# Projecting the first two token blocks of a hybrid attention layer one block at a time

## The chip, the cores and the metric

The kernel runs on one NeuronCore of a Trainium2 chip. The metric is the device time of one execution in microseconds (us). The program is one long, straight list of instructions for each engine: TensorE (PE; its weight loads are listed as PEld), VectorE (DVE), ScalarE (ACT), GpSimd (POOL) and the queue of SyncE (SP), which issues every transfer between memory and the chip.

## The reference

One layer of an encoder is applied to 2048 prompt tokens and 32 sample tokens. Its first half is what matters here:

```python
z = rmsnorm(x, g_attn) @ w_in            # 1024 -> 3072 columns
qa, ka, va, qb, kb, vb = split(z)        # group A: 512 columns each; group B: 512 columns each
oa = diff_attn(qa, ka, va, t5_bias, lam) # 4 heads, two maps of 64, values of 128, causal by chunks of 64
ob = band_attn(qb, kb, vb, clip_bias)    # 8 heads of 64, the own chunk of 64 and the 8 before it
h = x + concat(rms(oa), rms(ob)) @ w_out
```

After it come a squared-ReLU MLP, a gated per-layer embedding and a last norm. The sample tokens attend to 128 cached keys and to themselves. The new keys and values are outputs too.

## The kernel before

**Blocks.** The tokens lie in four blocks: blocks 0, 2 and 3 of 512 tokens, and block 1 of 512 prompt tokens and the 32 sample tokens. `HALVES` is [(0, 1), (2, 3)]. Every product is formed from values split in a high and a low part, as three matmuls (`mm3`, L211 to L213: high by high, high by low, low by high), accumulated over eight slices of 128 rows.

**`prep`** (L342) loads 128 tokens, squares and sums them, transposes them through PE (tiles `rp` and `xp`), scales them, stores `xT`, and writes the high and low halves `aH` and `aL` of the block, which stay on the chip until both groups have been projected.

**`wunit`** (L197) fetches one slice of weights of 512 KB (tile `wr`, two buffers) and splits it: ACT copies the high part `wh` (L189) and POOL subtracts the low part `wl` in four pieces of 256 columns (L184). `wh` and `wl` have three buffers each.

**`proj(half, grp, ...)`** (L381) projects the blocks in `half` for one group. It first takes two column slices of values, each of two weight units (PSUM tile `vps`; result through `vraw` and `vhl` to `vS`), and then for each of four `g` one slice of queries and one of keys (PSUM tile `qps`; results `qh`, `ql` to the scratch tensors `qS` and `kS` in memory). Its loops are ordered so:

```python
for c in vs:
    u = [self.wunit(wv[:, 4 * i : 4 * i + 4], [4, 256]) for i in range(2)]
    for b in half:
...
for g in gs:
    for kind in range(2):
        wh, wl = self.wunit(W[:, col : col + P].rearrange("(k p) c -> p k c", p=P), [8, P])
        for b in half:
```

So a slice is fetched and split once for each call, and serves all blocks of `half`. Keys are also transposed back for the output (`knat`, tile `ktp`, L471 and L480), in PSUM tiles that the argument `tp` gives: the call for group A passes the ring `ps_t`, the other calls pass the pool `mm`, which has two tiles and holds `vps` and `qps` too.

**`lam` and `biases`** (L254, L270) make lambda and the bias tables: two products on PE (tiles `pa`, `pb`), then rows written to memory and spread there to 128 rows for each head (`dba`, `dbb`).

**`attn_a(js, ...)`** (L534) is the attention of group A for the pairs of 128-query tiles in `js`; pair `j` covers tokens 256j to 256j + 255, and 8 stands for the sample tokens. For each head it loads the bias, the keys `ka` and the queries `q` from the scratch tensors, forms scores (`s`, L594), the softmax on DVE and ACT, transposes the weights through PE (`tpp`, L666) and multiplies by the values (`o`, L680 to L682). `JA0` is [(0, 1), (2, 3, 8)]: pairs 0 and 1 lie in block 0; pairs 2 and 3 and the samples lie in block 1 and see the keys of both blocks. `caches` (L491) brings the cached keys and values into the scratch tensors (tiles `ckn`, `ckh`, `ckl`) and must be done before the sample tokens.

**The order.** `run` (L1403) is traced in the order of its lines. A planner then puts the instructions of each engine in a fixed order: it runs a model of the engines in time, and whenever an engine is free it gives it the earliest instruction in the program whose inputs are ready by the model. So later work fills gaps of earlier work as far as its buffers are free, but on the chip each engine, and the SP queue, goes through its list strictly in that order. The part in question, L1433 to L1450, is: `prep` of blocks 0 and 1; `proj` of group A for both blocks; `lam` and `biases`; then `attn_a` for (0, 1), `caches`, `attn_a` for (2, 3, 8); then `proj` of group B for block 0, and after it for block 1, woven with `prep` of block 2. `prep` of block 2 is lifted to the rank that the program has at `mark` (L1443), but needs the buffers of block 0's activations.

Of the kernel before, what the change touches and what calls it, by code (L numbers as in the profile page):

```python
# [43 lines left out]
HALVES = [(0, 1), (2, 3)]  # L44
# [47 lines left out]
def drain(gen):  # L92
    for _ in gen:
        pass
# [57 lines left out]
class Kern:  # L152
# [1250 lines left out]
    def run(self):  # L1403
        tc, nc, a = self.tc, self.nc, self.a
        with ExitStack() as top:

            def opened(stack, name, bufs, space=None, side="left"):
                kw = {} if space is None else {"space": space}
                return stack.enter_context(
                    tc.tile_pool(name=name, bufs=bufs, side=side, reuse_waits="tile", **kw)  # L1410
                )
# [8 lines left out]
            mm = opened(psx, "mm", MM, PSUM)  # L1420
            tp = mm
            ps_s = opened(psx, "pss", 5 - MM, PSUM, "right")
            ps_t = opened(psx, "pst", 2, PSUM, "right")
# [4 lines left out]
            sg = opened(s12, "sg", 2)  # L1428
            self.consts(cp)
            with ExitStack() as x:  # L1430
                pp = opened(x, "pp0", 3, side="right")
                acts = {b: self.actpair() for b in HALVES[0]}
# [1 line left out]
                    drain(self.prep(b, acts, pp, ps_s, "s"))  # L1434
            ppx = ExitStack()
            pp = opened(ppx, "pp", 1)
            drain(self.proj(HALVES[0], 0, acts, sg, mm, Rings((ps_t, "tp"))))
            with ExitStack() as x:
                wk = opened(x, "setup", 1, side="right")
                self.lam(cp, wk)  # L1440
# [3 lines left out]
            with ExitStack() as x:  # L1444
                pool = opened(x, "a0", 1, side="right")
                for js in JA0:
                    if 8 in js:
                        self.caches(sg, tp)
                    self.attn_a(js, pool, ps_s, ps_t, ps_o)
            drain(self.proj((0,), 1, acts, sg, mm, tp))  # L1450
# [194 lines left out]
```

## Time and profile before

| quantity | value |
|---|---|
| median of 3 runs | 3224.73 us (3218.40 to 3230.53) |
| the profiled execution, its own time | 3224.94 us |
| span of the profile | 3223.1 us |
| granted TensorE clock, mean | 0.974 |
| busy: DVE, ACT, POOL | 1813.4, 1791.5, 1768.7 us |
| bytes moved | 579.89 MB, 180 GB/s over the span |

The profiled execution takes 1.84 us longer than its span, from the first to the last instruction. "Idle before" in a row of the profile is the time in which the engine waited ahead of that group of instructions, with the instruction or transfer whose end released it. In the rows by stretch, each engine has its busy microseconds and its count of instructions; PEclk is the granted clock of TensorE as a share of full speed; the DMA share is the mean busy share of the core's 16 DMA engines.

### The profile page before, as it was taken

Reading aid. Unit: us, or ns where it says so; the run is one execution under the profiler, and the core shown is the slowest. Engines: PE = TensorE matmul, PEld = TensorE weight load, DVE = VectorE, ACT = ScalarE, POOL = GpSimd, SP = SyncE. Lnnn points to the kernel's source line nnn. Section 1 sums busy time; section 2 is a strip of 40 time slices with the busy share of each in tenths; the row PEclk is TensorE's granted clock in tenths of the full one; section 3 lists DMA queues with packets and bytes.
Section 4 is the critical chain, followed back from the end, with each engine's and each line's share of the span. In section 5 each row is a group of like instructions: output and inputs, shape, how many; then the busy total and the mean of one; then the engine's idle time right before and its main releaser. Section 6 shows DMA issues by size and latency. Waiting matters only on the chain.

```text
span 3223.1 us, 51787 instructions
## 1 busy us (share of the span) xinstructions
PE 3019.3 (94%) x17497; PEld 2639.9 (82%) x17497; DVE 1813.4 (56%) x4270; ACT 1791.5 (56%) x3966; POOL 1768.7 (55%) x2451
## 2 busy tenths in 40 slices
PE   7989898999989999999999999998899999999997
PEld 6967788879878888788889999887788887888875
DVE  5126765444455454676675676235466665755845
ACT  4226665666566675676676776334354454444543
POOL 5427657443234544565564445657465567677751
PEclk9989899999999999999999999999999999999998
DMA  7578676987687854654564534456444468675611
GB/s 218 182 198 233 191 210 197 256 235 218 187 243 212 240 146 123 158 174 136 146 190 134 138 110 135 131 163 196 133 153 148 158 242 287 203 253 186 219 58 53
DMA packets 556257, 579.89 MB, mean 180 GB/s; under 512 B 41900, under 2 KB 412912, under 8 KB 555992
## 3 DMA queue, kind: packets, MB, share of 16 engines
q1 hardware_dynamic: 555992, 576.58, 59.7%
q8 instruction: 139, 2.28, 0.3%
q14 instruction: 126, 1.03, 0.1%
HBM read 438.37 MB, written 142.01 MB: 180 GB/s over the span
## 4 chain that ended last, share of the span: by engine, by line
PE 63%; DMA 11%; DVE 9%; ACT 4%; POOL 2%; issue 2%; SPq 1%; DVEq 0%; POOLq 0%; ACTq 0%
PE xps L211 3%; PE xps L212 3%; PE xps L213 3%; PE ups L211 3%; PE ups L212 3%; PE ups L213 3%; PE dps L211 3%; PE s L594 3%; PE dps L212 3%; PE dps L213 3%; PE dp L211 2%; PE dp L213 2%; PE dp L212 2%; PE ob L800 2%; PE gps L213 2%
## 5 line engine op out<-in xcount | busy, mean ns | idle before, releaser
L184 POOL TENSOR_TENSOR wl<-wr,wh 128x256 fp32r<-128x256 f32 x776 | 580.6, 780 | 463.3 <-ACT wh L189 405.4
L189 ACT ACTIVATE wh<-wr 128x1024 fp32r<-128x1024 f32 x258 | 272.6, 1057 | 259.4 <-PE dps L212 40.3
L211 PE MATMUL dps<-uh,wh 128*128 128x272 f32 (+1 forms) x768 | 265.4, 346 | 35.6 <-DVE h L982 27.7
L174 POOL TENSOR_TENSOR wl<-wr,wh 128x256 fp32r<-128x256 f32 x256 | 193.6, 787 | 170.5 <-ACT wh L189 170.3
L211 PE MATMUL ups<-cH,wh 128*128 128x272 f32 (+1 forms) x768 | 250.6, 327 | 2.7 <-ACT sqacc L913 1.5
L213 PE MATMUL dps<-uh,wl 128*128 128x272 f32 (+1 forms) x768 | 252.0, 328 | 0.0
L212 PE MATMUL dps<-ul,wh 128*128 128x272 f32 (+1 forms) x768 | 252.0, 328 | 0.0
L212 PE MATMUL ups<-cL,wh 128*128 128x272 f32 (+1 forms) x768 | 249.8, 325 | 1.2 <-POOL cL L174 1.2
L213 PE MATMUL ups<-cH,wl 128*128 128x272 f32 (+1 forms) x768 | 250.2, 326 | 0.0
L982 DVE TENSOR_TENSOR h<-h,dps 128x272 f32<-128x272 f32 (+1 forms) x384 | 195.9, 514 | 90.9 <-PE dps L213 88.7
L211 PE MATMUL qps<-aH,wh 128*128 128x512 f32 (+1 forms) x640 | 229.3, 358 | 8.8 <-DVE a L368 3.6
L213 PE MATMUL qps<-aH,wl 128*128 128x512 f32 (+1 forms) x640 | 229.0, 358 | 0.0
L212 PE MATMUL qps<-aL,wh 128*128 128x512 f32 (+1 forms) x640 | 228.5, 357 | 0.0
L594 PE MATMUL s<-ka,q 128*128 128x512 f32 (+3 forms) x768 | 188.9, 350 | 37.0 <-ACT e L608 19.3
L211 PEld LDWEIGHTS dps<-uh,wh 128*128 128x128 f32 x768 | 148.5, 193 | 60.6 <-DVE h L982 40.0
L608 ACT ACTIVATE e<-s,nm 128x384 f32<-128x384 f32 (+3 forms) x256 | 154.6, 609 | 64.5 <-DVE nm L600 42.6
L600 DVE TENSOR_REDUCE nm<-s 128x1 f32<-128x512 f32 (+3 forms) x256 | 147.4, 587 | 61.1 <-PE s L594 60.0
L212 PE MATMUL dp<-dx,dw 128*128 128x512 f32 x448 | 177.5, 396 | 0.7 <-DVE dx L195 0.7
L174 POOL TENSOR_TENSOR dw<-dv,dw 128x256 fp32r<-128x256 f32 x160 | 149.2, 961 | 49.1 <-ACT dw L189 39.8
L211 PE MATMUL dp<-dx,dw 128*128 128x512 f32 x448 | 174.7, 396 | 0.0
L594 PEld LDWEIGHTS s<-ka,q 128*128 128x128 f32 x768 | 128.3, 196 | 54.3 <-ACT e L608 24.3
L213 PE MATMUL dp<-dx,dw 128*128 128x512 f32 x448 | 171.5, 396 | 0.0
(273 smaller groups left out, 9593.9 us busy)
## 6 DMA issues: line engine op xcount, KB each, us to landing
wd<-w_down SPq DMA_DIRECT2D x96, 512.0 KB, 5.4
wr<-w_in SPq DMA_DIRECT2D x74, 512.0 KB, 5.5
q<-qS SPq DMA_DIRECT2D x256, 128.0 KB, 4.1
v<-vSa SPq DMA_DIRECT2D x64, 512.0 KB, 4.4
wr<-w_up SPq DMA_DIRECT2D x64, 512.0 KB, 4.3
wr<-w_down SPq DMA_DIRECT2D x64, 512.0 KB, 4.0
ut<-uS SPq DMA_DIRECT2D x56, 512.0 KB, 4.1
ka<-kS SPq DMA_DIRECT2D x32, 512.0 KB, 8.0
```

Of the source, the lines that this page charges most:

```text
L174: nc.gpsimd.tensor_tensor(out[:, sl], a[:, sl], b[:, sl], op=op)
L184: nc.gpsimd.tensor_tensor(out[:, sl], a[:, sl], b[:, sl], op=op)
L189: nc.scalar.activation(hi, raw, AF.Copy)
L211: nc.tensor.matmul(ps, lh, rh, start=start and i == 0, stop=False)
L212: nc.tensor.matmul(ps, lh, rl, start=False, stop=False)
L213: nc.tensor.matmul(ps, ll, rh, start=False, stop=stop and i == n - 1)
L594: nc.tensor.matmul(s, q[:, m, hl, P * qi : P * qi + nr], kt[:, m, k0 - kb : k0 - kb + n], start=hl == 0, stop=hl == 1)
L600: nc.vector.tensor_reduce(nmx, s, axis=AX.X, op=ALU.max, negate=True)
L608: nc.scalar.activation(dst, src, AF.Exp, bias=nmx, accum_out=z[:nr, m, bi : bi + 1])
L800: nc.tensor.matmul(o[:, qa:qb], vt, pt[:kn, i - kfirst, qa:qb], start=x == 0 and y == 0, stop=x == len(order) - 1 and y == 1,)
L982: nc.vector.tensor_tensor(hv, hv, ps, op=ALU.add)
```

## The change

The one call of `proj` for group A on both blocks becomes two calls of one block each. The call for block 0 stays where the old one was. The call for block 1 stands after the first attention, (0, 1), has been issued, ahead of `caches`, and passes `tp` (the pool `mm`) for the transposed keys. Every weight slice of group A is thus fetched and split once for block 0 and once more for block 1: 12 units (four of values, four of queries, four of keys) come in a second time.

```diff
             ppx = ExitStack()
             pp = opened(ppx, "pp", 1)
-            drain(self.proj(HALVES[0], 0, acts, sg, mm, Rings((ps_t, "tp"))))
+            drain(self.proj((0,), 0, acts, sg, mm, Rings((ps_t, "tp"))))
             with ExitStack() as x:
                 wk = opened(x, "setup", 1, side="right")
                 self.lam(cp, wk)
...
                 for js in JA0:
                     if 8 in js:
+                        drain(self.proj((1,), 0, acts, sg, mm, tp))
                         self.caches(sg, tp)
                     self.attn_a(js, pool, ps_s, ps_t, ps_o)
             drain(self.proj((0,), 1, acts, sg, mm, tp))
```

## What was predicted

> **What bounds the kernel now.** I read the page first, for the bound of the whole.
>
> ```profile
> span 3223.1 us, 51787 instructions
> PE 3019.3 (94%) x17497; PEld 2639.9 (82%) x17497; DVE 1813.4 (56%) x4270; ACT 1791.5 (56%) x3966; POOL 1768.7 (55%) x2451
> PE 63%; DMA 11%; DVE 9%; ACT 4%; POOL 2%; issue 2%; SPq 1%; DVEq 0%; POOLq 0%; ACTq 0%
> ```
>
> PE is busy for 94% of the span and no other engine for more than 56%. The edit changes no matmul: each weight slice meets the same columns of activations, only in two visits. So PE's work stays, and the time can change only by PE's idle time, by its clock, or by other engines that make it wait. I therefore asked for the stretches in which the moved work lies.
>
> ```profile
> core 0: us, PE busy (x) PEld busy (x) DVE busy (x) ACT busy (x) POOL busy (x), PEclk, DMA share, GB/s
> 0.00:20.00 20.00, 6.81 (x30) 5.94 (x30) 8.73 (x32) 12.18 (x31) 8.16 (x17) 1.00 0.79 234
> 20.00:40.00 20.00, 15.07 (x114) 14.19 (x112) 14.72 (x44) 11.62 (x33) 15.90 (x22) 1.00 0.93 295
> 40.00:60.00 20.00, 16.07 (x116) 15.16 (x117) 15.46 (x52) 8.73 (x25) 13.28 (x19) 0.90 0.59 183
> 60.00:180.00 120.00, 118.95 (x799) 109.72 (x799) 18.68 (x46) 28.37 (x53) 52.03 (x78) 0.99 0.53 172
> 180.00:200.00 20.00, 15.87 (x83) 10.38 (x81) 3.56 (x7) 3.68 (x7) 7.87 (x13) 0.91 0.60 190
> 200.00:220.00 20.00, 16.91 (x137) 16.27 (x138) 1.90 (x4) 4.74 (x8) 3.33 (x6) 1.00 0.99 260
> 220.00:240.00 20.00, 11.67 (x53) 9.78 (x51) 10.50 (x53) 9.81 (x37) 5.25 (x9) 0.59 0.79 193
> 240.00:320.00 80.00, 75.63 (x429) 64.96 (x429) 51.30 (x184) 51.71 (x156) 56.69 (x82) 0.98 0.84 234
> 320.00:400.00 80.00, 62.78 (x436) 58.39 (x436) 63.08 (x193) 55.90 (x170) 48.50 (x70) 0.87 0.68 191
> 400.00:540.00 140.00, 127.32 (x967) 120.81 (x966) 97.78 (x318) 96.64 (x289) 86.94 (x142) 0.99 0.70 201
> 540.00:560.00 20.00, 15.79 (x66) 12.39 (x65) 7.15 (x16) 6.21 (x12) 17.08 (x27) 0.91 0.68 206
> ```
>
> There are four stages. Until 60 us the two blocks are prepared, and PE idles 13.19 + 4.93 + 3.93 = 22.05 us. From 60 to 180 us PE runs projection alone and is full. From 180 to 240 us comes a passage to the attention, with 4.13 + 3.09 + 8.33 = 15.55 us idle. From 240 to 540 us attention and group B's projection mix, with 4.37 + 17.22 + 12.68 = 34.27 us idle.
>
> That decides how the edit must be judged. It moves block 1's projection out of the full stage and uses it to fill the attention. But the attention is filled already, by group B's projection, and that filler would then be left over and run by itself later. Moving filler from one place to another gains nothing where PE is full at both. Only the idle microseconds above are to be had.
>
> **How much moves.**
>
> ```profile
> 60.00:93.40 33.40, 32.35 (x258) 0.96 0.54 175
> 93.40:191.80 98.40, 94.80 (x576) 1.00 0.52 170
> ```
>
> These are the rows of the value tiles and of the query and key tiles alone. One value tile of 24 matmuls costs 33.40 / 258 x 24 = 3.1 us; block 0 has 4 tiles in each of 2 slices (25 us), block 1 has 5 (31 us). The 8 slices of queries and keys take 98.40 us, 12.3 each, for 512 columns of block 0 and 544 of block 1: 48 and 50 us. So block 0 holds 73 us of PE, block 1 81 us, and block 0 alone should be through at about 192 - 81 = 111 us.
>
> **Term 1, the second fetch and split: +0.**
>
> ```profile
> L189 ACT ACTIVATE wh<-wr 128x1024 fp32r<-128x1024 f32 x12 | 12.7, 1057 | 22.9 <-PE qps L212 16.7 <-PE vps L213 2.9 <-PE qps L213 2.4
> L184 POOL TENSOR_TENSOR wl<-wr,wh x48: 720/738/872, 68.0 to 193.1; 128x256 fp32r<-128x256 f32 x48
> L184 POOL TENSOR_TENSOR wl<-wr,wh x16: 717/761/1141, 319.8 to 399.8; 128x256 fp32r<-128x256 f32 x16
> wr<-w_in SPq DMA_DIRECT2D x5, 512.0 KB, 6.6
> wr<-w_in SPq DMA_DIRECT2D x12, 512.0 KB, 4.1
> ```
>
> Twelve more units cost ACT 12 x 1.057 = 12.7 us, POOL 48 x 0.738 = 35.4 us, and the DMA engines 6 MB (12 issues on SP). They fall beside block 1's 81 us of PE and the attention, where POOL is busy 56.69 of 80 us with a block's 12 units already among them, as group B's block 0 is now the filler. The load is therefore of a kind that this stage bears today, and I cost it at nothing. What cover there is in the first stage is a question of rhythm: with block 0 alone, a slice feeds PE for 6 us rather than 12.3. A unit takes 4.1 to 6.6 us to land (the medians of 60 to 200 us and of 0 to 60 us), 1.06 on ACT and 4 x 0.738 = 2.95 on POOL, 8.1 to 10.6 us; two buffers for `wr` give one unit every 4.1 to 5.3 us. That is under 6.0, by 0.7 us at the worst. If it isn't, the cover is gone: see the second rival.
>
> The Trainium skill (GPSIMD Engine Reference, Specifications) says that POOL shares its interfaces to the on-chip memory with VectorE and contends with VectorE's instructions that read two inputs there, which speaks against moving POOL's subtractions beside attention. The two POOL rows above bear it out weakly: with VectorE quiet a piece takes 0.738 us, in the stretch with VectorE at 79% 0.761. By the rows the rule costs 48 x 0.023 = 1.1 us of a POOL that has room; the page gives no figure.
>
> **Term 2, the first 60 us: -4.**
>
> ```profile
> PE rp L356 <- DVE rsy L225: 12.4, 4, 10.8
> ```
>
> Of the 22.05 us idle, 10.8 pass before the first transpose and stay. In the other 11.3 us, PE waits for block 1's tiles, because the first value slice holds two of three `wh` buffers until all nine tiles have passed, and the next slice's second unit can't be split. With block 0 alone the slice is released after four tiles, and the next slices can fill. But POOL is already busy 15.90 + 13.28 of the 40 us from 20 to 60, which leaves 10.8 us, room for 3 units of 2.95. The bounds are 0 and -11; I take -4, because the DMA share of 0.93 from 20 to 40 us delays the units too.
>
> **Term 3, the passage to the attention: -5.** The chain of waits is quoted first, then SP's own list.
>
> ```profile
> 192.46 1.29 PE pa L281 x2
> 204.19 9.49 DMA dbb<-rb
> 213.70 8.29 DMA q<-qS
> 222.13 0.66 PE s L594 x2
> 234.83 5.04 DMA ka<-kS
> 239.96 1.62 PE s L594 x6
> ```
>
> ```profile
> 222.26 2.31 SPq L165 DMA_DIRECT2D kS<-ckh  x4
> 224.91 2.42 SPq L165 DMA_DIRECT2D kS<-ckl  x4
> 227.43 0.39 SPq L165 DMA_DIRECT2D kS<-ckh  x1
> 230.49 1.54 SPq L165 DMA_DIRECT2D kS<-ckh  x3
> 232.12 1.34 SPq L165 DMA_DIRECT2D kS<-ckl  x3
> 234.83 0.58 SPq L165 DMA_DIRECT2D ka<-kS  x1
> ```
>
> From the bias products to the first scores pass 30 us. This chain moves whole, to about 111 to 141 us, and block 1's values (31 us) cover it as group B's (25 us) do now. But one thing drops out: 15 stores of the cached keys stand in SP's list ahead of the second head's keys, 2.31 + 2.42 + 0.39 + 1.54 + 1.34 = 8.0 us of issuing, and PE then waits for exactly these keys.
>
> ```profile
> PE s L594 <- DMA ka<-kS: 4.4, 1, 4.4
> ```
>
> `caches` now comes behind block 1's projection, since it uses the same buffers, so these stores leave this place. The bounds are 0 (block 1's own loads and stores take the place) and -13 (all 8.33 us idle from 220 to 240, and the 0.41 of 11.67 us that the granted clock of 0.59 lost there, 4.8). I take -5, near the 4.4 us of the wait.
>
> The row of 0.59 has a rule beside it: the Trainium skill (TensorE: Matmul & The Clock Gate, What's actually happening) says that PE's clock is halved after an idle window of about 3.4 us and comes back after as long a busy one. The trace agrees. By that rule a wait of 4.4 us that goes would return up to 1.7 us more, -6.7 instead of -5; one that the change adds would cost as much more.
>
> **Term 4, the attention and its new fillers: +1.** The 34.27 us idle there belong to the attention's own steps.
>
> ```profile
> L594 PE MATMUL s<-ka,q 128*128 128x256 f32 (+3 forms) x232 | 53.1, 337 | 21.3 <-DMA ka<-kS 8.4 <-DMA q<-qS 7.5 <-ACT e L608 4.9
> L471 PE MATMUL ktp<-ident,kr 128*128 128x128 f32 x32 | 5.0, 274 | 1.1 <-ACT kr L455 1.1
> ```
>
> The loads of `ka` and `q` and the exponentials are the same in number, and wait in the same SP list. I leave them at 0, between -17 (all of 320 to 400 us) and +17 (as much again). Block 1's transposed keys now pass through `mm`, two tiles that `qps` needs too; before, the eight of them (32 transposes) cost 1.1 us of idle. With 4 of block 1's and 4 of the samples' in `mm`, a wait of 1.1 each is the upper bound, 8.8; 0 the lower; I take +1, since scores can run in between. The stores of `caches` reappear before (2, 3, 8), under group B's projection, at nothing; if it can't cover them, they cost their 4.4 us there. Everything behind 540 us keeps its fillers; 81 us of group B's projection run alone where the first group ran alone before.
>
> **Sum.** 0 - 4 - 5 + 1 = -8 us, against the profiled execution's own 3224.94 us, which is 0.21 us from the median of 3224.73: 3217 us. This kernel's measurement can tell about 0.5%, 16 us, from no change, so I forecast no change that can be told.
>
> **Rival A, faster: the attention is relieved.** The worst stretch is 320 to 400 us, where `prep` of block 2 mixes with the start of (2, 3, 8) and VectorE is 79% busy. After the change block 2's preparation must wait until group B has passed block 0, which comes later against the attention. If this stretch closes wholly (-17.22) along with the passage's rows from 200 to 240 (-3.09 - 8.33), the time is 3224.94 - 28.6 = 3196 us. For it: DVE and ACT are nearly idle in the 120 us of pure projection. Against it: PE's waits there name loads of `q` and `ka`, which stay.
>
> **Rival B, slower: the weights come too slowly for one block.** The page shows one place where one block is projected with new slices: 540 to 560 us, block 2. POOL is busy 17.08 of 20 us there and PE idles 4.21 us, 21%. The point is where a unit holds its `wr` buffer over 12 us (2 buffers x 6.0), 1.4 us more than the 10.6 above; POOL's queue of `aL` pieces could add that. If 21% holds for block 0's 73 us and block 1's first 31 us, it costs 22 us and eats the gains: 3247 us.
>
> **Rival C: the planner gives it back.** It orders the whole program anew by its model; block 1's work may go in so that attention starts little earlier, or later passages may come out worse. With the gains gone and nothing lost but the 4.4 us of the cached keys: 3229 us.
>
> **How the numbers follow.** The forecast gets 0.55, its own range 3204 to 3230 (terms 2 and 3 at their better halves; or both at 0 with 5 us lost in `mm`). Rival A gets 0.19, B 0.17, C 0.09. Over 0.5% faster means below 3208.6: A and 0.08 of the forecast, 0.27. Slower means above 3240.9: B and a little of C, 0.18. Within: 0.55. The range from 3193 to 3245 takes in A with 3 us to spare and the lower half of B, and leaves out some 0.15.
>
> **What would show it.** Right: PE's busy time within 1% of 3019 us; block 0's last `qps` near 111 us and the first scores near 135 to 141, not 222; no `kS<-ckh` ahead of the second `ka`; group A's early attention over about 81 us sooner, followed by projection alone; POOL up by 35 us and ACT by 13. Wrong: PE idle behind POOL `wl` or DMA `wr` in the first 110 us (rival B); far less than 17 us idle where (2, 3, 8) begins (rival A); first scores still near 200 us (rival C).

## The result, and the profile after

| | before | after |
|---|---|---|
| median of 4 runs | 3226.80 us | 3202.62 us (3200.24 to 3206.47) |
| the profiled execution, its own time | 3224.94 us | 3206.47 us |
| span of the profile | 3223.1 us | 3204.7 us |
| granted clock, mean | 0.974 | 0.978 |

The changed kernel takes 0.9933 of the time before, with a 95% interval from 0.9911 to 0.9956: 22 us less (the two medians alone differ by 24.2 us). The prediction said 3217 us, within 3193 to 3245.

These are the rows of the page of the changed kernel that answer to the first ones of before; the last is the group of POOL's subtractions for the weights.

```profile
span 3204.7 us, 51871 instructions
PE 3004.1 (94%) x17497; PEld 2629.7 (82%) x17497; DVE 1821.3 (57%) x4270; ACT 1799.2 (56%) x3978; POOL 1802.4 (56%) x2499
L184 POOL TENSOR_TENSOR wl<-wr,wh 128x256 fp32r<-128x256 f32 x824 | 614.7, 777 | 435.0 <-ACT wh L189 367.7
```

PE has the same 17497 matmuls. Its idle time (span less busy) went from 203.8 to 200.6 us, only 3.2 us of the 18.4 us by which the spans differ. The other 15.2 us are busy time, 3019.3 to 3004.1: the same matmuls, fewer of them at a lowered clock. The clock's means say the same: 0.026 x 3223.1 = 83.8 us missing before, 0.022 x 3204.7 = 70.5 after. In the two traces the clock stands either at full or at half, and PE is busy for 119.8 us at half before and for 94.4 us after. Half of that difference, 12.7 us, is an estimate of the clock's part in the 15.2 us.

The stretches of the first 460 us, with the columns as before:

```profile
core 0: us, PE busy (x) PEld busy (x) DVE busy (x) ACT busy (x) POOL busy (x), PEclk, DMA share, GB/s
0.00:20.00 20.00, 6.24 (x25) 5.13 (x26) 7.96 (x31) 11.79 (x30) 7.38 (x16) 1.00 0.77 225
20.00:40.00 20.00, 16.68 (x130) 15.31 (x128) 15.14 (x44) 13.41 (x33) 17.27 (x23) 1.00 0.95 303
40.00:60.00 20.00, 16.87 (x125) 15.78 (x126) 16.38 (x46) 11.18 (x28) 19.07 (x26) 1.00 0.79 239
60.00:120.00 60.00, 60.00 (x315) 48.26 (x314) 13.97 (x34) 16.71 (x28) 40.06 (x56) 1.00 0.75 231
120.00:140.00 20.00, 7.64 (x53) 6.81 (x51) 1.67 (x10) 3.14 (x7) 6.43 (x10) 0.74 1.02 260
140.00:160.00 20.00, 17.45 (x112) 16.65 (x112) 11.82 (x56) 12.13 (x44) 5.87 (x10) 0.75 1.02 255
160.00:180.00 20.00, 17.73 (x137) 16.81 (x135) 13.16 (x48) 12.39 (x40) 13.50 (x19) 0.93 0.68 205
180.00:460.00 280.00, 250.03 (x1736) 231.43 (x1735) 190.44 (x607) 184.96 (x553) 177.07 (x268) 0.96 0.73 208
```

PE is full, with projection alone, only until 120 us now. The passage to the attention now lies from 120 to 180 us, and PE idles 12.36 + 2.55 + 2.27 = 17.2 us in it, against 15.55 before, with the DMA engines full. PE's longest wait there, and from SP's list ahead of it the spreading transfers and the loads for the first head:

```profile
PE s L594 <- DMA q<-qS: 13.3, 2, 12.1
```

```profile
112.22 2.49 SPq L165 DMA_DIRECT2D dba<-ra  x4
118.58 5.72 SPq L165 DMA_DIRECT2D dbb<-rb  x8
124.34 0.61 SPq L165 DMA_DIRECT2D ba<-dba  x1
125.15 1.34 SPq L165 DMA_DIRECT2D ka<-kS  x2
127.14 4.88 SPq L165 DMA_DIRECT2D q<-qS  x4
```

Last, the first and last start (the two numbers ahead of the shapes) of the scores of group A, those of the samples, the first scores of group B, and the first product behind the MLP's first part (`xps`); first before, then after.

```profile
L594 PE MATMUL s<-ka,q x768: 221/338/792, 222.1 to 1960.2; 128*128 128x256 f32 x68, 128*128 128x384 f32 x64, 128*128 128x512 f32 x52, 128*128 128x128 f32 x8
L594 PE MATMUL s<-ks,q x16: 236/237/318, 356.9 to 504.7; 128*32 128x160 f32 x16
L760 PE MATMUL sb<-kbt,q x464: 222/309/635, 566.5 to 1247.8; 128*128 128x320 f32 x125, 128*32 128x160 f32 x8, 128*128 128x128 f32 x6, 128*128 128x512 f32 x6
L211 PE MATMUL xps<-Xb,wc x192: 388/394/796, 2299.7 to 2613.7; 128*128 128x512 f32 x192
```

```profile
L594 PE MATMUL s<-ka,q x768: 221/338/794, 137.7 to 1898.4; 128*128 128x256 f32 x68, 128*128 128x384 f32 x64, 128*128 128x512 f32 x52, 128*128 128x128 f32 x8
L594 PE MATMUL s<-ks,q x16: 235/237/260, 273.9 to 428.3; 128*32 128x160 f32 x16
L760 PE MATMUL sb<-kbt,q x464: 221/309/773, 489.6 to 1177.9; 128*128 128x320 f32 x125, 128*32 128x160 f32 x8, 128*128 128x128 f32 x6, 128*128 128x512 f32 x6
L211 PE MATMUL xps<-Xb,wc x192: 392/394/795, 2277.7 to 2591.6; 128*128 128x512 f32 x192
```

The first half's attention runs 76 to 84 us sooner. At `xps`, where both kernels have nearly the same work behind them, the changed one is 22.0 us ahead, and it loses 3.6 of them again by the end.

**Where the 22 us were won.** Between the start and `xps` the two kernels do their work in different orders, so equal times are not equal progress. I therefore measured what PE has lost up to a time. For every kind of matmul (tile and shape) I took the lower quartile, over the traces of this study, of the time from its start to the start of the next one (0.23 us for 512 columns, 0.12 for 256). The sum of these over all matmuls that have started is the time that the work needs; the time passed less this sum is lost, whether by idling or by a lowered clock. One trace of each kernel enters; where two kernels have the same order, their sums at 100 us differ by up to 1.3 us. Telling the kinds apart by their inputs too moves single entries by up to 7 us, and differences from the kernel before by up to 2.6 us. The traced execution lies up to 7.5 us (e4) from the median of its kernel, so a few us between two rows mean nothing. The whole table stands here, with the experiments that follow; each share is against executions of the kernel before taken beside it, with medians of 3226.03 us (e1 to e4), 3230.14 us (e5, e7, p5) and 3226.89 us (e8 to e11); "moved" are kernels in which block 1's projection stands behind the first attention.

| kernel | time as a share of before | lost to 100 us | 100 to 560 | 560 to 2400 |
|---|---|---|---|---|
| before | 1 | 36.2 | 100.6 | 214.6 |
| after (moved) | 0.9933 [0.9911, 0.9956] | 28.9 | 107.9 | 192.0 |
| e1_two_calls | 0.9882 [0.9865, 0.9900] | 29.3 | 100.1 | 185.4 |
| e2_caches_first (moved) | 0.9942 [0.9926, 0.9959] | 29.6 | 109.6 | 196.1 |
| e3_ktp_own_ring (moved) | 0.9979 [0.9963, 0.9994] | 28.6 | 110.9 | 209.5 |
| e4_before_ktp_mm | 0.9901 [0.9884, 0.9918] | 38.8 | 91.1 | 185.5 |
| e5_bias_early (moved) | 0.9825 [0.9807, 0.9843] | 29.2 | 98.9 | 177.8 |
| e7_two_calls_bias_early | 0.9938 [0.9925, 0.9950] | 29.2 | 100.9 | 202.3 |
| p5_before_sample_first | 0.9944 [0.9933, 0.9956] | 37.5 | 98.8 | 200.6 |
| p5_after_sample_first (moved) | 0.9928 [0.9916, 0.9941] | 28.4 | 99.7 | 200.4 |
| e8_values_by_block | 0.9930 [0.9914, 0.9945] | 34.0 | 102.1 | 189.5 |
| e9_spread_later (moved) | 0.9888 [0.9868, 0.9908] | 28.6 | 100.8 | 180.8 |
| e10_both (moved) | 0.9890 [0.9872, 0.9908] | 28.5 | 99.8 | 178.0 |
| e11_before_spread_later | 0.9978 [0.9966, 0.9990] | 35.6 | 102.4 | 206.7 |

In the changed kernel the first 100 us lose 7.3 us less, the stretch to 560 us loses 7.3 us more, and 22.6 us are won from 560 to 2400 us, where the edit touches nothing. Of this late stretch, PE's idle time falls from 97.6 to 89.2 us, and its busy time at half the clock from 64.3 to 45.5 us: 8.4 us of the late gain are idle time, and by an estimate 9.4 (half of 18.8) the clock.

### The profile page after: what moved, and what is told of

Read it like the earlier page. It is cut to its first block, busy times and chain, and to the rows that moved or that the text cites. A ratio compares the mean times of both kernels' runs of the same rounds, so it can differ in the third digit from the quotient of the medians.

```text
span 3204.7 us, 51871 instructions
## 1 busy us (share of the span) xinstructions
PE 3004.1 (94%) x17497; PEld 2629.7 (82%) x17497; DVE 1821.3 (57%) x4270; ACT 1799.2 (56%) x3978; POOL 1802.4 (56%) x2499
## 4 chain that ended last, share of the span: by engine, by line
PE 51%; DVE 6%; DMA 5%; ACT 2%; issue 2%; POOL 1%; SPq 1%; DVEq 0%; POOLq 0%; ACTq 0%
PE ups L212 3%; PE ups L211 3%; PE ups L213 3%; PE xps L211 3%; PE xps L212 3%; PE xps L213 3%; PE dps L211 3%; PE dps L213 3%; PE dps L212 3%; PE dp L211 2%; PE dp L212 2%; PE dp L213 2%; PE s L594 2%; PE gps L213 2%; PE gps L212 2%; PE gps L211 2%
## 5 line engine op out<-in xcount | busy, mean ns | idle before, releaser
L184 POOL TENSOR_TENSOR wl<-wr,wh 128x256 fp32r<-128x256 f32 x824 | 614.7, 777 | 435.0 <-ACT wh L189 367.7
L189 ACT ACTIVATE wh<-wr 128x1024 fp32r<-128x1024 f32 x270 | 285.3, 1057 | 307.2 <-PE dps L212 51.8
L211 PE MATMUL dps<-uh,wh 128*128 128x272 f32 (+1 forms) x768 | 264.7, 345 | 29.2 <-DVE h L982 24.3
L174 POOL TENSOR_TENSOR wl<-wr,wh 128x256 fp32r<-128x256 f32 x256 | 194.7, 792 | 152.0 <-ACT wh L189 152.0
L608 ACT ACTIVATE e<-s,nm 128x512 f32<-128x512 f32 (+3 forms) x256 | 154.6, 608 | 81.7 <-DVE nm L600 53.8
```

The lines of the kernel that those rows point to most:

```text
L174: nc.gpsimd.tensor_tensor(out[:, sl], a[:, sl], b[:, sl], op=op)
L184: nc.gpsimd.tensor_tensor(out[:, sl], a[:, sl], b[:, sl], op=op)
L189: nc.scalar.activation(hi, raw, AF.Copy)
L211: nc.tensor.matmul(ps, lh, rh, start=start and i == 0, stop=False)
L608: nc.scalar.activation(dst, src, AF.Exp, bias=nmx, accum_out=z[:nr, m, bi : bi + 1])
```

## The experiments

Two theories stood against each other. Theory 1: the early gain comes from the second call alone, and the large late one from the new order in which the planner puts everything that follows. Theory 2: the move pays, because the attention starts earlier and is covered better.

**e1: the second call without the move.**

```diff
-            drain(self.proj(HALVES[0], 0, acts, sg, mm, Rings((ps_t, "tp"))))
+            for b in HALVES[0]:
+                drain(self.proj((b,), 0, acts, sg, mm, Rings((ps_t, "tp"))))
```

> The kernel before, with block 0 and block 1 projected for group A in two calls, each slice split twice, and nothing moved: both calls stand ahead of the bias tables and the attention. Theory 1 (the first-stage gain comes from releasing the first value slices after four tiles; the rest of the gain is the planner's new order of what follows, not the move): PE's idle time from 0 to 100 us falls by about 7 us as in the changed kernel; past 560 us its idle time differs from the kernel before by up to 10 us either way; total 3209 to 3227. Theory 2 (the move itself pays, since the attention starts 84 us earlier): the same 7 us at the start, past 560 us as in the kernel before within 3 us, total about 3219, and no more than a third of the 22 us gained. Rival B of the prediction (weights too slow for one block): idle PE behind POOL wl or DMA wr between 60 and 190 us, total 3230 or more.

Measured: 3186.93 us, 39 us less than before and less than the changed kernel. Its stretches to 60 us, to 100 us and over its passage:

```profile
0.00:60.00 60.00, 40.65 (x276) 37.88 (x277) 38.71 (x117) 36.34 (x90) 42.52 (x63) 0.97 0.82 253
60.00:100.00 40.00, 40.00 (x186) 32.30 (x185) 10.80 (x27) 12.95 (x21) 31.86 (x46) 1.00 0.78 238
180.00:240.00 60.00, 44.75 (x259) 37.24 (x257) 18.98 (x81) 20.27 (x62) 18.15 (x30) 0.77 0.85 229
```

PE idles 19.35 us in the first 60 us (22.05 before) and is full behind, so the early gain is there without the move, and rival B (weights too slow for one block) is refuted: up to 190 us no wait of PE for a weight is listed. The passage lies where it lay before and PE idles as much in it (15.25 us). Theory 2 allowed a third of the gain; this kernel has more than the whole of it. The total lies below what theory 1 allowed too: 29 us of it come from 560 to 2400 us.

**e2: the cached keys back at the start of the attention (changed kernel).**

```diff
-                        drain(self.proj((1,), 0, acts, sg, mm, tp))
                         self.caches(sg, tp)
+                        drain(self.proj((1,), 0, acts, sg, mm, tp))
```

> The changed kernel with the cached keys and values brought in ahead of block 1's projection, so that their stores stand in SP's list near the start of the attention again. Term 3 of the prediction: PE waits about 4 us longer before the second head's scores, total about 3207. If these stores never mattered: the passage as in the changed kernel, total 3202 by theory 2 (move pays); by theory 1 (new order of what follows) anything from 3195 to 3215 with the difference past 560 us.

Measured: 3208.93 us; its interval overlaps that of the changed kernel. These rows of SP's list in its passage show stores of the cached keys ahead of the second head's keys again:

```profile
145.31 2.71 SPq L165 DMA_DIRECT2D kS<-ckl  x4
148.12 1.81 SPq L165 DMA_DIRECT2D kS<-ckh  x4
150.97 0.58 SPq L165 DMA_DIRECT2D ka<-kS  x1
```

Up to 180 us it has lost 71.7 us, the changed kernel 56.1, but by 560 us the difference is 2.4. So `caches` at this place costs 15.6 us there, more than term 3 said, and most of it comes back. That the stores themselves do it is not shown: the second head's keys are issued no later than in the changed kernel (150.97 against 151.66 us), and PE's longest waits up to 180 us name `q` (9.7 us), copies of block 0's keys ahead of their transposes (`kr`, 4.0) and nothing that the profile shows (3.7).

**e3: block 1's transposed keys in the attention's ring (changed kernel).**

```diff
-                        drain(self.proj((1,), 0, acts, sg, mm, tp))
+                        drain(self.proj((1,), 0, acts, sg, mm, Rings((ps_t, "tp"))))
```

> The changed kernel with block 1's transposed keys in the attention's transpose ring, as the kernel before had them, not in the two tiles that the projection uses. Term 4 of the prediction: 1 us faster, at most 9, by PE's waits in the projection of block 1; slower if the attention's transposes then wait for the ring. Theory 2: total 3193 to 3204 and past 560 us like the changed kernel within 3 us. Theory 1: past 560 us up to 10 us either way, total 3190 to 3215.

Measured: 3217.45 us, 15 us slower than the changed kernel, above both expectations. To 560 us it loses 2.7 us more; the rest lies behind, 209.5 against 192.0. No gain from taking the keys out of `mm` is seen.

**e4: the transposed keys in the projection's tiles (kernel before).**

```diff
-            drain(self.proj(HALVES[0], 0, acts, sg, mm, Rings((ps_t, "tp"))))
+            drain(self.proj(HALVES[0], 0, acts, sg, mm, tp))
```

> The kernel before with the transposed keys of both blocks in the two tiles of the projection; no work is added, removed or moved in the program's order. In the first 190 us it can cost 0 to 9 us (term 4 priced it at 1.1 us for each of eight). Theory 2 (what follows is worth what its place in the program makes it): past 560 us as the kernel before within 3 us, total 3224 to 3236. Theory 1 (any edit of the order makes the planner order what follows anew, with a spread of several us): past 560 us up to 10 us either way.

Measured: 3193.75 us, 32 us less than before, by one argument. I had thought of it as nearly neutral, and it is not. The bias products `pa` and group A's scores, in the kernel before (first row) and in this one:

```profile
L281 PE MATMUL pa<-oa,ta x2: 651/746/842, 192.5 to 192.9; 32*4 32x384 f32 x2
```

```profile
L281 PE MATMUL pa<-oa,ta x2: 477/478/478, 76.2 to 76.5; 32*4 32x384 f32 x2
L594 PE MATMUL s<-ka,q x768: 223/338/796, 143.8 to 1913.0; 128*128 128x256 f32 x68, 128*128 128x384 f32 x64, 128*128 128x512 f32 x52, 128*128 128x128 f32 x8
```

The bias products, the transposed keys and the attention's transposes take their tiles in turn from the same ring of two. In the kernel before, `pa` comes in that ring behind the last transposed keys, and so it waits until group A is projected, at 192.5 us; with the keys out of the ring it runs at 76.2 us and the attention starts at 143.8 us, although nothing was moved in the program. Both theories had set the late stretch within 10 us of the kernel before; it loses 29.1 us less. The changed kernel had this in it unseen: only block 0's keys stand in the ring ahead of `pa`.

**e5 and e7: the bias tables ahead of the projection,** in the changed kernel and in e1.

```diff
+            with ExitStack() as x:
+                wk = opened(x, "setup", 1, side="right")
+                self.lam(cp, wk)
+                self.biases(wk, ps_t)
             drain(self.proj((0,), 0, acts, sg, mm, Rings((ps_t, "tp"))))
-            with ExitStack() as x:
-                wk = opened(x, "setup", 1, side="right")
-                self.lam(cp, wk)
-                self.biases(wk, ps_t)
```

> The changed kernel with lambda and the bias tables traced ahead of block 0's projection, so that their chain (products, rows to memory, spreading over 128 rows) runs under the projection. If the passage to the attention waits for that chain and its 12 spreading transfers (PE waits 12.1 us for q in the changed kernel, and the granted clock is halved for 20.5 us), the passage gets 10 to 20 us cheaper: PE idle from 100 to 560 us falls from 58 to 40 or 48, total 3183 to 3193 if what follows is unchanged, 10 more either way if the planner orders it anew. If the wait is for the transfers of block 1's projection and the attention itself, the passage stays within 4 us and only what follows moves the total.

> Two calls, both ahead of the attention, not moved, and the bias tables ahead of them. Theory: the passage costs the unmoved kernels as much as the moved ones (PE's idle time from 180 to 240 us is 15.6 us before), so it gets cheaper here by 10 us too: total 3177, 10 either way by the planner's order. If the move is what makes an early bias table pay, no gain: 3187.

Measured: e5 3177.00 us, the fastest kernel here, 0.9825 of before and clear of the changed kernel's interval; e7 3211.48 us, slower than e1. First a stretch of e5 and its group A's scores, then rows of e7:

```profile
100.00:560.00 460.00, 417.35 (x2913) 388.65 (x2912) 279.76 (x956) 292.68 (x851) 261.38 (x416) 0.94 0.81 229
```

```profile
L594 PE MATMUL s<-ka,q x768: 220/338/792, 121.0 to 1862.9; 128*128 128x256 f32 x68, 128*128 128x384 f32 x64, 128*128 128x512 f32 x52, 128*128 128x128 f32 x8
```

```profile
L594 PE MATMUL s<-ka,q x768: 222/338/795, 124.5 to 1939.5; 128*128 128x256 f32 x68, 128*128 128x384 f32 x64, 128*128 128x512 f32 x52, 128*128 128x128 f32 x8
L666 PE MATMUL tpp<-ident,e x552: 188/272/421, 202.1 to 1959.1; 128*128 128x128 f32 x181, 32*128 32x32 f32 x2, 32*32 32x32 f32 x1
```

In e5 PE idles 42.65 us from 100 to 560 us, as expected (58.13 in the changed kernel). The passage is not all that e5 wins: against the changed kernel it loses 9.0 us less to 560 us and 14.2 us less behind. In e7 the expectation failed: the first scores come at 124.5 us, but the first transposes of the attention only at 202.1, since they stand in the ring behind the keys of block 1. The early table is worth nothing while the ring holds the next step.

**p5: the same instructions in another order,** in the kernel before and in the changed one.

```diff
-JA0 = [(0, 1), (2, 3, 8)]
+JA0 = [(0, 1), (8, 2, 3)]
```

> The kernel before with the sample tokens taken ahead of pairs 2 and 3 for each head, (8, 2, 3) in place of (2, 3, 8): the same instructions in another order, nothing moved between stages, the plan unchanged up to the second attention. Theory 1 (the planner's order of what follows is worth up to 15 us either way, whatever the edit): the first 200 us unchanged, the total off 3226 by 5 to 30 us. Theory 2 (only real changes of work or place move the time): total within 5 us of 3226.

> The changed kernel with the sample tokens ahead of pairs 2 and 3. Theory 1: the first 180 us as in the changed kernel, the total off 3202 by 5 to 30 us either way. Theory 2: within 5 us of 3202, perhaps some us slower where the cached keys must be there sooner.

Measured: 3215.02 us, 0.56% less than before, and 3208.62 us, which is not to be told from the changed kernel. The first trace has PE's first 1707 instructions, up to 314 us, in the order of before; then the order is another, and 14 us of the loss between 560 and 2400 us are gone. So an edit that only swaps the order of two parts of one attention wins 5/6 of what the change wins, as theory 1 expected. In the second trace the stretch to 560 us loses 8.2 us less than in the changed kernel and the one behind 8.4 us more, so this run does not decide between the theories.

**e8: only the value slices block by block (kernel before).**

```diff
-            drain(self.proj(HALVES[0], 0, acts, sg, mm, Rings((ps_t, "tp"))))
+            for b in HALVES[0]:
+                drain(self.proj((b,), 0, acts, sg, mm, Rings((ps_t, "tp")), gs=()))
+            drain(self.proj(HALVES[0], 0, acts, sg, mm, Rings((ps_t, "tp")), vs=()))
```

> The kernel before, with only the value slices of group A taken block by block (4 units split twice), the query and key slices shared as before, nothing moved. If term 2's reason is right (the first value slice holds two of three buffers until all nine tiles are through), PE idles 2 to 4 us less in the first 100 us, near the 19 to 20 us of the kernels with two calls against 23.1 before. If it is the query and key slices that fill the first stage, no change there. The total can move by 15 us either way with the planner's order behind it: 3211 to 3241.

Measured: 3205.55 us. Its two stretches to 100 us:

```profile
0.00:60.00 60.00, 41.64 (x294) 39.58 (x295) 39.88 (x118) 36.05 (x90) 43.94 (x64) 0.97 0.83 257
60.00:100.00 40.00, 35.55 (x271) 33.14 (x270) 12.00 (x33) 9.53 (x20) 28.76 (x41) 1.00 0.68 211
```

To 60 us PE idles 18.36 us, less than with two whole calls: the value slices are what held it up there. From 60 to 100 us it idles 4.45 us where e1 and the changed kernel have none. The expectation of 2 to 4 us over 100 us failed (22.8 against 23.1): block 0's queries and keys are needed to keep what the value slices win.

**e9, e10, e11: group B's spreading transfers later,** in the changed kernel, in e5 and in the kernel before. The loop of 8 transfers (`dbb`, L301) is taken out of `biases` into a function of its own.

```diff
+            self.spread_b()
             drain(self.proj((0,), 1, acts, sg, mm, tp))
```

> The changed kernel with the 8 spreading transfers of group B's bias table (384 KB each) traced ahead of group B's projection, so that they no longer stand in SP's list ahead of the first keys and queries. Theory: they are what PE waits for at 120 to 137 us (s behind q, 12.1 us), so that wait falls to 5 us or less, the half-clock stretch of 20.5 us shrinks, and PE idles 5 to 10 us less between 100 and 560 us than the 58.1 of the changed kernel. Rival: the wait is the chain from the bias products through memory to the first head's table, and stays at 8 us or more. Total 3180 to 3205.

> The changed kernel with the bias tables ahead of block 0's projection and group B's spreading transfers later. If the passage is only these two things, the first scores come at 115 us or sooner (121.0 with the early tables alone) and PE idles 36 to 43 us between 100 and 560 us (42.6 with the early tables alone); total 3165 to 3190, since what follows is ordered anew.

> The kernel before with group B's spreading transfers later. If they hold up the passage without the move as well, first scores come 7 to 9 us sooner than 222 us and PE idles 4 to 8 us less between 180 and 240 us than 15.6. Total 3205 to 3228 with the planner's order.

Measured: 3190.22, 3191.07 and 3220.38 us. The wait for `q` in the passage of e9 (the lines of its kernel stand 3 lower) and its stretch to 560 us:

```profile
PE s L597 <- DMA q<-qS: 3.0, 1, 3.0
```

```profile
100.00:560.00 460.00, 412.91 (x2892) 382.42 (x2891) 279.93 (x958) 291.63 (x846) 261.18 (x410) 0.94 0.81 228
```

The wait falls from 12.1 to 3.0 us, and PE idles 47.1 us instead of 58.1: the changed kernel's passage did wait for these transfers, and the rival (the chain itself) falls. Of e9's gain on the changed kernel, 11.2 us lie past 560 us and are no price of that wait. In e10 the first scores start at 108.8 us, as expected, but PE idles 48.9 us to 560 us, not 36 to 43, and the total is no better than e9's and just past the 3190 us expected. In e11 the scores start at 212.0 us, 10 us sooner than before, and PE's idle time from 180 to 240 us falls from 15.55 to 11.62 us, just short of the 4 to 8 us expected; by 560 us nothing of it is left (102.4 against 100.6 lost).

## Why the prediction was right, and where it was not

The time lies in the range and the direction is right; the size is not. The forecast was -8 us and no change that can be told; measured are -22 us, just beyond the 16 us that were set as the bound. That the direction came out right is luck: up to 560 us, where all four terms lie, what is won and what is lost cancel (-7.3 and +7.3 us), and the whole gain lies behind, in a stretch that the sum held at nothing.

- **The bound and the place of the work: right.** Block 0's last `qps` is through at 103.7 us (111 forecast), first scores at 137.7 (135 to 141), the samples' last scores 76 us sooner (81 forecast), PE's matmuls the same, POOL up by 33.7 us (35). ACT rose by 7.7 us, not 13; its weight copies alone rose by 12.7.
- **Term 1, +0: right.** In the first 120 us no wait of PE for a weight is listed, and POOL's mean piece stayed at 777 ns (780 before). The 40 pieces from 120 to 240 us, beside the attention, have a median of 734 ns, no more than the 738 ns with VectorE quiet. The Trainium skill (GPSIMD Engine Reference, Specifications) says that POOL and VectorE share an interface and contend when VectorE's instructions read two inputs there; this trace shows no such cost.
- **Term 2, -4: right in sign, without the clock.** Nine kernels with two whole calls lose 28.4 to 29.6 us in the first 100 us, five with one call 34.0 to 38.8; before against after it is -7.3, inside the bounds of 0 and -11. But the term counted idle time, and that fell by only 2.9 us (23.1 to 20.2); the rest is in the main the clock, at which the term didn't look: before, PE is busy for 6.8 us of these 100 us at half the clock, after for none. e8 bears out the reason to 60 us, and shows that behind it the new queries and keys are needed too.
- **Term 3, -5: wrong.** "I take -5, near the 4.4 us of the wait" failed: the stores left, but the passage did not get cheaper. PE idles 17.2 us there (15.55) and has 0.74 and 0.75 of its clock from 120 to 160 us, so the passage costs more than its idle time. I had the spreading transfers in the quoted chain (`dbb`, 9.49 us) and took them as moving along unchanged. But block 0 alone ends with the DMA engines busier (0.75 from 60 to 120 us, 0.53 from 60 to 180 us before), and behind the transfers `q` came 12.1 us late. e9 takes them away and the wait falls to 3.0. The Trainium skill (TensorE: Matmul & The Clock Gate, What's actually happening) says that the clock is halved after an idle window of about 3.4 us; the trace agrees, with 20.5 us at half the clock that begin within the wait of 12.1 us.
- **Term 4, +1: not to be told.** From 180 to 460 us PE idles 29.97 us, with the attention that had 34.27 from 240 to 540. e3 shows no gain from another ring.
- **"Everything behind 540 us keeps its fillers": the step that failed.** It was costed at 0, and -22.6 us came there. Group B's attention starts at 489.6 us, not at 566.5 as that step implies, since of the 81 us of "projection alone" only some 30 are left (460 to 489 us) and the rest fills the attention. Rival C named the planner's new order as something that can only take away; here it gave. Rival A's total, 3196 us, is close to the measured one by another way: the passage it wanted closed stayed, and the attention won 4.3 us of idle time, not 17.

**What made the late gain.** Theory 2 falls as the cause: without the move, e1 and e4 win more than the changed kernel, and in p5_before the order alone wins 14 us of that stretch. The losses from 560 to 2400 us run from 177.8 to 209.5 us in the seven moved kernels and from 185.4 to 214.6 us in the seven others; the kernel before has the largest of all fourteen. Whether the move has some share in the late gain cannot be told: the means of the two groups are 190.7 and 197.8 us, and each spreads over some 30 us. So theory 1 stands in this form: an edit in the first 300 us makes the planner lay out the next 2000 anew, that is worth some 15 us either way, and the kernel before had a poor draw. This is argued from the spread and from p5_before, and not shown for the changed kernel itself, for the two late gains do not lie in the same place. From 560 to 1250 us and from 1250 to 2270 us PE idles 31.0 and 54.4 us in the kernel before, 33.6 and 44.0 in the changed one, 24.8 and 56.5 in p5_before: the change wins in the second stretch, the reordering in the first. What in the layout of the kernel before is poor stays open: its waits are spread over many short ones, and no run fixed the late order while changing the early one.

## What to carry to other kernels

Where a planner lays out the whole program, compare a change with a few reorderings that add and remove no work, before its mechanism gets the credit: here such a reordering was worth 0.56%. Follow what stands in line ahead of the first step of a stage, in the list of transfers and in the turn of a small ring of tiles: the ring's last users, not the data, held the bias products back by over 100 us. Splitting weights again for each block made PE wait for no weight here, where POOL had room; the move together with an early bias table (e5) came to 1.75%, of which most, 36.8 us against the kernel before, again lies past 560 us.

## What the runs showed of the hardware

PE's time can change without its work and nearly without its idle time: of the 18.4 us between the spans, 15.2 us are busy time of the same 17497 matmuls, which ran for 119.8 us at half the clock before and for 94.4 us after. The 20 us with a wait of 12.1 us had 0.74 of the clock, and the 20 us behind them 0.75. The DMA engines at a share of 1.02 moved 255 to 260 GB/s in the passage, and 303 GB/s at 0.95 in the preparation, so a full share isn't one rate.
